# Other piece widths for the channel-major products, a norm split in two, and an output projection in three PSUM banks

## The chip, the cores and the metric

The kernel runs on one core of a Trainium2 chip. The metric is the device time of one execution in microseconds. TensorE is called PE here, VectorE DVE, ScalarE ACT, GpSimd POOL, and SyncE, whose queue issues nearly all DMA transfers, SP.

## The reference

One layer of a hybrid decoder for 1024 prompt tokens and 8 × 8 sample tokens (1088 in all), with model width 1024:

```python
h = rmsnorm(x, g_mix);  proj = h @ w_in            # 1024 -> 3328 columns
o_rw = rwkv7_mixer(...)       # 4 heads of 64: token shift, low-rank gates, matrix-state recurrence, bonus
o_cv = short_conv_mixer(...)  # pb * conv3(pc * px), 256 channels
o_sb = stick_breaking(...)    # 8 heads of 64; sample tokens attend to a paged cache of 512 as well
x = x + concat(o_rw, o_cv, o_sb) @ w_out
h2 = rmsnorm(x, g_mlp)
x = x + square(relu(h2 @ w_up)) @ w_down           # 1024 -> 4096 -> 1024
gate = sigmoid(rmsnorm(x, g_ple) @ w_ple_gate)
x = x + gate * (p @ w_ple_proj)                    # p: 256 wide, one row for each token
```

The new keys, values, recurrence states, shift rows and convolution rows are outputs too.

## The kernel before

All large products take fp32 operands split into a high part (fp32r) and the rest, and each k-step is three matmuls: high × high, high × low, low × high (L169 to L171 in `gemm_t`, L795 to L797 in `project`, L1094 to L1096 in `gemm_p`). ACT makes the high part with a cast, POOL or DVE the low part with a subtraction: for weights that is L158 and L159 in the first half, L1074 and L1075 in the second.

**First half, products by channel.** The loop at the start normalizes x tile by tile (128 tokens; h is L193), transposes it on PE (L198) and evicts the high part on ACT (L200) and the low part on DVE (L201). A channel-major product (`gemm_t`) makes 128 channels for all 1088 tokens, weights stationary. It goes in three pieces, given by `CH`, each with a PSUM bank of its own and 24 matmuls:

```python
CH = ((0, 384), (384, 384), (768, 320))
```

`rw_tile` does that for the eight 128-channel tiles of the recurrence and evicts each piece with L330 (copy) and L333 (scaled copy); the convolution does it for six. The low-rank gates, the squared norms of kk and the bonus of the recurrence use the same pieces. The bonus is L446 (a product with a block of ones) and L447 (the product times vx, in place in xs), three of each in a row. `wkv_base` solves the triangular systems of the recurrence on DVE: it loads base_Z from DRAM (L277) and goes through steps of L284 and L286. Its result is stored (L288), and each chunk of the recurrence loads its operands ar and bk (L487, L490) and then multiplies them (L512).

**First half, products by token.** `project` makes queries, keys and values: two token tiles with 256 columns each in one bank. ACT copies the bank (L802) and squares it into sq (L805, one buffer), and DVE makes the norms. L848 and L849 split and L852 stacks rows in DRAM; L828 stores keys.

**Second half.** Tokens 0 to 511 are group A, 512 to 1087 group B (two chunks of 288). A `Part` holds the residual x of a group. `out_proj` multiplies with w_out, 24 matmuls a piece, and DVE adds each piece to x (L1406). The order is: A's MLP blocks up to 13, `out_proj(B)`, A's last blocks, B's MLP with seven products of halves in place of eight (`seven`, L1446 to L1448), then A's gates in the loop over `gate(A, sl)`, between whose pieces B's operands are made, and last B's gates (`gate7`; L1596 to L1599 in `gated`).

`Part.rms` makes 1/rms of a group's tokens: ACT squares the eight slices of x, POOL and DVE add them up (L1329), DVE adds the last two (L1330, the tile `sums`); PE sums over the partitions with one-column matmuls (L1338), ACT and DVE take root and reciprocal, and PE (L1347) and ACT spread them over all partitions into `rb`. Each gate is multiplied with rb first (L1596). `ple_inputs` loads the rows of p (L1583), transposes them (L1586) and splits them. `gate7_weights` loads the weights of B's gates and makes their sums of blocks on DVE (L1430 to L1433).

**What sets the order.** A scheduler places the instructions when the program is built: each engine has one queue and goes through it in order, and the scheduler fills the queues by the order of the code and by times that it simulates for each instruction. A size that changes moves instructions far from its own line. PSUM has eight banks, and `banks(...)` hands out the named ones in turn; `acc` is banks 0, 1 and 2.

Of the kernel before, what the change touches and what calls it, by code (L numbers as in the profile page):

```python
# [33 lines left out]
NJ = 8  # L34
NS = NB * NJ
T = NP + NS
CH = ((0, 384), (384, 384), (768, 320))
C0 = math.exp(-0.5)
RMS_EPS = 1e-6
GN_EPS = 64e-5  # L40
# [8 lines left out]
def hybrid_step(ctx: ExitStack, tc: tile.TileContext, I, O):  # L49
# [6 lines left out]
    def f(t):  # L56
        return t.bitcast(F32)
# [9 lines left out]
    def banks(*ids):  # L67

        turn = itertools.cycle(ids)

        def take():
            i = next(turn)
            return psum.tile([128, 512], F32, name=f"b{i}", bufs=1)

        return take
# [67 lines left out]
    class Weights:  # L143
# [3 lines left out]
        def load(self, src, nk=8, ncol=256, tag="w", sub=None):  # L147
            wh = self.pool.tile([128, nk * ncol], F32R, name="wh", tag=tag + "h", bufs=2)
            wl = self.pool.tile([128, nk * ncol], F32R, name="wl", tag=tag + "l", bufs=2)
            wh3, wl3 = (w[:, :nk * ncol].rearrange("p (k c) -> p k c", k=nk) for w in (wh, wl))  # L150
            step = max(1, 1024 // ncol)
            for k0 in range(0, nk, step):
                n = min(step, nk - k0)
                raw = self.pool.tile([128, 1024], F32, name="wr", bufs=2)
                r3 = raw[:, :n * ncol].rearrange("p (k c) -> p k c", k=n)
                SP.dma_start(r3, src[k0 * 128:(k0 + n) * 128, :].rearrange("(k p) c -> p k c", p=128))
                flat = slice(k0 * ncol, (k0 + n) * ncol)
                S.copy(wh[:, flat], raw[:, :n * ncol])  # L158
                (sub or G).tensor_sub(wl[:, flat], raw[:, :n * ncol], f(wh[:, flat]))  # L159
            return wh3, wl3  # L160
# [67 lines left out]
    for s in range(2):  # L228
        hs = slice(64 * s, 64 * s + 64)
        for q in range(2):  # L230
            for kind in range(2):
                m = mfull[hs, q, kind, :]
# [86 lines left out]
    def rw_tile(w, m, ct):  # L319
# [5 lines left out]
        G.tensor_copy(rs3[:, :, 0], shT[:, ct, :])  # L325
        for t0, n in CH:
            ps = acc()
# [16 lines left out]
    def lora(dst, i, j, prods, func, bias):  # L344
        c = slice(j * 128, j * 128 + 128)
        for t0, n in CH:
            ps = tr()
# [29 lines left out]
    for j in range(2):  # L377
# [14 lines left out]
        for a in range(2):  # L392
            rb = pe_tile("rb", F32R)
            rbs.append((rb, rp.tile([128, 2, 64], F32R, name=f"rb8{a}")))
            for d, i0, i1 in ((rb[:, :1024], 0, 8), (rbs[a][1].rearrange("p s d -> p (s d)"), 8, 9)):
# [4 lines left out]
                else:  # L400
                    h = rbs[0][0][:, :1024] if i0 == 0 else rbs[0][1].rearrange("p s d -> p (s d)")
                    V.tensor_sub(d, src, f(h).rearrange("p (i s d) -> p i s d", i=i1 - i0, s=2))
        for t0, n in CH:
            ps = tr()
# [38 lines left out]
        SP.dma_start(ar_s[2, j], vx[:, t_])  # L443
        for t0, n in CH:
            ps = tr()
# [529 lines left out]
    def convolution():  # L975
# [5 lines left out]
        for j in range(2):  # L981
            t = cv.tile([128, LW], F32, name="cc", bufs=2)
            cc.append(t)
            for t0, n in CH:
                ps = gemm_cv()
# [4 lines left out]
        for j in range(2):  # L990
# [6 lines left out]
            S.copy(us3[:, :, 0:2], pt[:, :16].rearrange("p (b i) -> p b i", i=2))  # L997
            for t0, n in CH:
                ps = gemm_cv()
# [89 lines left out]
    def gemm_p(ps, w, m, x, t0, n, nk=8, ks=None):  # L1089

        xh, xl = x
        for k in ks or range(nk):
            a, b = xh[k // 4][:, k % 4, t0:t0 + n], xl[k // 4][:, k % 4, t0:t0 + n]
            PE.matmul(ps[:, :n], w(0, k, m), a, start=(k == 0), stop=False)  # L1094
            PE.matmul(ps[:, :n], w(0, k, m), b, start=False, stop=False)  # L1095
            PE.matmul(ps[:, :n], w(1, k, m), a, start=False, stop=(k == nk - 1))  # L1096
# [167 lines left out]
    class Part:  # L1264
# [56 lines left out]

        def rms(self, bank, wide=False):

            sums, sq = self.act("sums", F32), [self.act("sq", F32) for _ in range(2)]
            for m in range(8):
                t = sums[:, m] if m < 2 else sq[m // 2 % 2][:, m % 2]
                S.square(t, self.x[:, m])
                if m >= 2:
                    (G, V)[m % 2].tensor_add(sums[:, m % 2], sums[:, m % 2], t)  # L1329
            V.tensor_add(sums[:, 0], sums[:, 0], sums[:, 1])  # L1330
            self.rb = self.pool.tile([128, self.n], F32, name="rb", bufs=1)
            if not wide:

                n, ni = self.n, len(self.tiles)
                ps = bank()
                for i in range(ni):
                    e = min(n, 128 * i + 128)
                    PE.matmul(ps[:, i:i + 1], sums[:, 0, e - 128:e], onesq[:, 0:1], start=True, stop=True)  # L1338
                rs = self.pool.tile([128, ni], F32, name="rs", bufs=2)
                S.activation(rs, ps[:, :ni], AF.Sqrt, bias=eps_rms, scale=1.0 / D)  # L1340
                V.reciprocal(rs, rs)
                for t0 in range(0, n, 512):
                    r = min(512, n - t0)
                    ps = bank()
                    for i in range(t0 // 128, -(-(t0 + r) // 128)):
                        c = min(128, n - 128 * i)
                        PE.matmul(ps[:, 128 * i - t0:128 * i - t0 + c], rs[:, i:i + 1].to_broadcast([128, 128]),  # L1347
                                  ident[:, 128 - c:], start=True, stop=True)
                    S.copy(self.rb[:, t0:t0 + r], ps[:, :r])
            else:  # L1350
                for t0, n in self.chunks:
                    ps = bank()
                    PE.matmul(ps[:, :n], onesq, sums[:, 0, t0:t0 + n], start=True, stop=True)
                    S.activation(self.rb[:, t0:t0 + n], ps[:, :n], AF.Sqrt, bias=eps_rms, scale=1.0 / D)
                    V.reciprocal(self.rb[:, t0:t0 + n], self.rb[:, t0:t0 + n])
# [41 lines left out]
    def out_proj(p, k0=0, nk=8, bank=acc, order=None):  # L1397
        nm = 16 // nk
        x = [h[k0 // 4:] for h in p.h]
        for m0 in order or range(0, 8, nm):  # L1400
            w = load(w_out[k0 * 128:(k0 + nk) * 128, m0 * 128:(m0 + nm) * 128], nk, nm * 128)
            for m in range(m0, m0 + nm):
                for t0, n in p.chunks:
                    ps = bank()
                    gemm_p(ps, w, m - m0, x, t0, n, nk=nk)
                    V.tensor_add(p.x[:, m, t0:t0 + n], ps[:, :n], p.x[:, m, t0:t0 + n])  # L1406

    def up(p, fb, bank=acc):
        w = load(w_up[:, fb * 256:fb * 256 + 256], 8, 256)
        ah, al = p.act("ah", F32R), p.act("al", F32R)  # L1410
        for m in range(2):
            for t0, n in p.chunks:
                ps = bank()
                gemm_p(ps, w, m, p.h, t0, n)
                r = p.tmp("r")
                V.scalar_tensor_tensor(r[:, :n], ps[:, :n], 0.0, p.rb[:, t0:t0 + n], op0=ALU.max, op1=ALU.mult)
                S.square(r[:, :n], r[:, :n])
                S.copy(ah[:, m, t0:t0 + n], r[:, :n])
                V.tensor_sub(al[:, m, t0:t0 + n], r[:, :n], f(ah[:, m, t0:t0 + n]))  # L1419
        return p, fb, ah, al  # L1420
# [119 lines left out]
    B = Part(mpb, mpb, mpb, 512, 576, ((0, 288), (288, 288)))  # L1540
# [6 lines left out]
        u, before = up(A, fb), u  # L1547
        down(*before)
    late = banks(0, 1, 2, 3, 4, 5)
    out_proj(B, bank=late, order=(0, 4, 2, 6))  # L1550
    u, before = up(A, NA - 1, late), u
    down(*before, bank=late)
    B.rms(banks(6, 7))
# [74 lines left out]
    def gate(p, sl):  # L1628
        w = load(wg_[:, sl * 256:sl * 256 + 256], 8, 256)
        w2_ = load(wp_[:, sl * 256:sl * 256 + 256], 2, 256)  # L1630
        if sl == 3:

            ps_ = [acc() for _ in range(2)]
            for ks in (range(0, 4), range(4, 8)):
                for m2 in range(2):
                    gemm_p(ps_[m2], w, m2, p.h, 0, p.n, ks=ks)
        for m2 in range(2):
            for t0, n in p.chunks:
                if sl == 3:
                    ps = ps_[m2]  # L1640
                else:
                    ps = acc()
                    gemm_p(ps, w, m2, p.h, t0, n)
                end = gated(p, w2_, m2, 2 * sl + m2, t0, n, ps[:, :n], B.tmp("g")[:, :n])
            finish(p, 2 * sl + m2)
            yield end
# [46 lines left out]
    for m, end in enumerate(itertools.chain.from_iterable(gate(A, sl) for sl in range(4))):  # L1693
        with tc.issue_after(end.ins):
            if m < 3:
                B.operands("g_ple", (2, 3, 1, 4), mpb, 4, ks=((0, 1), (2,), (3,))[m], out=ops)
            if m == 2:
                B.rms(banks(3, 4))
            if m == 3:
                ple_inputs(B, banks(5, 7))  # L1700
        if m == 6:
            w = {}
            pieces = gate7_weights(0, w)
            for _ in range(5):
                next(pieces)
# [38 lines left out]
```

## Time and profile before

| | us |
|---|---|
| median of 3 runs (1706.22 to 1711.11) | 1706.24 |
| the profiled execution | 1715.32 |
| its span | 1713.5 |
| PE busy | 1641.7 |
| DVE, ACT, POOL busy | 1106.7, 821.3, 726.1 |

The span runs from the first instruction to the last; the rest of the profiled execution's time lies outside of it. Rows of a timeline give the start in us, the duration in us, the engine, the line, the operation, output and inputs with their shapes, and in brackets the idle time of the engine just before with what ended it. Matmuls overlap, so the pace of PE is read from start to start. A row "PE b L795 <- ACT sq L805: 5.4, 1, 5.4" says that PE waited for that ACT instruction 5.4 us in all, once, and 5.4 at the longest.

### The profile page before, as it was taken

Reading aid. Unit: us, or ns where it says so; the run is one execution under the profiler, and the core shown is the slowest. Engines: PE = TensorE matmul, PEld = TensorE weight load, DVE = VectorE, ACT = ScalarE, POOL = GpSimd, SP = SyncE. Lnnn points to the kernel's source line nnn. Section 1 sums busy time; section 2 is a strip of 40 time slices with the busy share of each in tenths; the row PEclk is TensorE's granted clock in tenths of the full one; section 3 lists DMA queues with packets and bytes.
Section 4 is the critical chain, followed back from the end, with each engine's and each line's share of the span. In section 5 each row is a group of like instructions: output and inputs, shape, how many; then the busy total and the mean of one; then the engine's idle time right before and its main releaser. Section 6 shows DMA issues by size and latency. Waiting matters only on the chain. (4 is left out here: it accounts for less than half of the span.)

```text
span 1713.5 us, 30844 instructions
## 1 busy us (share of the span) xinstructions
PE 1641.7 (96%) x11853; PEld 1479.4 (86%) x11853; DVE 1106.7 (65%) x1918; ACT 821.3 (48%) x1627; POOL 726.1 (42%) x778
## 2 busy tenths in 40 slices
PE   6999999999999898999999999999999999999998
PEld 5899988889888777888886777987999999999788
DVE  6266844555267759888854335277777777765896
ACT  6633433344344657666643344473443334437653
POOL 4123121123132565443334564366655455538631
PEclk9999999999999999999999999999999999999999
DMA  5134466335523764444235565322332322323332
GB/s 189 51 117 126 142 166 166 72 83 137 169 62 102 219 182 125 117 131 124 77 107 173 159 179 173 127 86 83 90 94 81 98 87 87 100 74 105 88 118 55
DMA packets 212373, 202.27 MB, mean 118 GB/s; under 512 B 58305, under 2 KB 177761, under 8 KB 212098
## 3 DMA queue, kind: packets, MB, share of 16 engines
q1 hardware_dynamic: 202498, 179.33, 35.4%
q0 software_dynamic: 5120, 16.78, 3.4%
q10 hardware_dynamic: 4608, 4.20, 1.0%
q8 instruction: 93, 1.52, 0.4%
q14 instruction: 54, 0.44, 0.1%
HBM read 163.27 MB, written 36.98 MB: 117 GB/s over the span
## 5 line engine op out<-in xcount | busy, mean ns | idle before, releaser
L1075 POOL TENSOR_TENSOR wl<-wr,wh 128x512 fp32r<-128x512 f32 x182 | 256.1, 1418 | 261.8 <-ACT wh L1074 208.5
L1074 ACT CAST wh<-wr 128x512 fp32r<-128x512 f32 x308 | 187.9, 621 | 310.9 <-PE b L1095 211.3
L1515 DVE TENSOR_TENSOR x<-b,x 128x288 f32<-128x288 f32 (+1 forms) x384 | 199.5, 529 | 96.4 <-PE b L1096 95.1
L1094 PE MATMUL b<-ah,wh 128*128 128x288 f32 (+1 forms) x768 | 253.8, 331 | 3.2 <-DVE x L1515 2.2
L1096 PE MATMUL b<-ah,wl 128*128 128x288 f32 (+1 forms) x768 | 252.6, 329 | 0.0
L1095 PE MATMUL b<-al,wh 128*128 128x288 f32 (+1 forms) x768 | 252.4, 329 | 0.0
L1094 PEld LDWEIGHTS b<-ah,wh 128*128 128x128 f32 x768 | 144.5, 188 | 15.4 <-DVE x L1515 4.6
L1096 PEld LDWEIGHTS b<-ah,wl 128*128 128x128 f32 x768 | 144.7, 188 | 10.2
L1095 PEld LDWEIGHTS b<-al,wh 128*128 128x128 f32 x768 | 144.8, 189 | 9.3 <-DVE al L1419 0.3
L795 PE MATMUL b<-wh,h_hi 128*128 128x256 f32 x432 | 128.2, 297 | 5.4 <-ACT sq L805 5.4
L1094 PE MATMUL b<-nh,wh 128*128 128x512 f32 x320 | 128.2, 401 | 2.8 <-DVE x L1406 1.6
L797 PE MATMUL b<-wh,h_lo 128*128 128x256 f32 x432 | 127.6, 295 | 0.0
L1095 PE MATMUL b<-nl,wh 128*128 128x512 f32 x320 | 127.4, 398 | 0.0
L1096 PE MATMUL b<-nh,wl 128*128 128x512 f32 x320 | 127.3, 398 | 0.0
L796 PE MATMUL b<-wl,h_hi 128*128 128x256 f32 x432 | 125.4, 290 | 0.0
L1075 DVE TENSOR_TENSOR wl<-wr,wh 128x512 fp32r<-128x512 f32 x126 | 105.2, 837 | 27.3 <-ACT wh L1074 24.4
L159 POOL TENSOR_TENSOR wl<-wr,wh 128x1024 fp32r<-128x1024 f32 x26 | 64.5, 2495 | 126.3 <-ACT wh L158 126.3
L169 PE MATMUL b<-h_hi,wh 128*128 128x384 f32 (+1 forms) x336 | 115.3, 343 | 1.9 <-ACT xs L333 1.3
L170 PE MATMUL b<-h_lo,wh 128*128 128x384 f32 (+1 forms) x336 | 114.2, 340 | 0.3 <-DVE h_lo L201 0.3
L171 PE MATMUL b<-h_hi,wl 128*128 128x384 f32 (+1 forms) x336 | 112.9, 336 | 0.0
L922 DVE TENSOR_TENSOR_SCAN keep<-keep,onesq 128x128 f32<-128x128 f32 (+3 forms) x64 | 95.6, 1494 | 21.4 <-POOL keep L920 20.7
L1446 PE MATMUL b<-op,wh 128*128 128x288 f32 x320 | 95.0, 297 | 3.1 <-DVE c L1596 1.8
(437 smaller groups left out, 4451.7 us busy)
## 6 DMA issues: line engine op xcount, KB each, us to landing
wr<-in_w_up SPq DMA_DIRECT2D x64, 512.0 KB
wr<-in_w_down SPq DMA_DIRECT2D x64, 512.0 KB
wr<-in_w_in SPq DMA_DIRECT2D x26, 512.0 KB
wr<-in_w_out SPq DMA_DIRECT2D x16, 512.0 KB
wr<-in_w_ple_gate SPq DMA_DIRECT2D x16, 512.0 KB
xt<-in_x_prompt SPq DMA_DIRECT2D x8, 512.0 KB
stk_s<-sth ACTq DMA_DIRECT2D x32, 128.0 KB
stk_s<-stl SPq DMA_DIRECT2D x32, 128.0 KB
```

The lines of the kernel that those rows point to most:

```text
L169: PE.matmul(ps[:, :n], wh[:, k, c], a, start=(k == 0), stop=False)
L170: PE.matmul(ps[:, :n], wh[:, k, c], b, start=False, stop=False)
L171: PE.matmul(ps[:, :n], wl[:, k, c], a, start=False, stop=(k == nk - 1))
L795: PE.matmul(o, a, w[0][:, k, :], start=(k == 0), stop=False)
L796: PE.matmul(o, a, w[1][:, k, :], start=False, stop=False)
L797: last = PE.matmul(o, b, w[0][:, k, :], start=False, stop=(k == 7))
L1074: S.copy(h3, src)
L1075: (sub or G).tensor_sub(l3, src, f(h3))
L1094: PE.matmul(ps[:, :n], w(0, k, m), a, start=(k == 0), stop=False)
L1095: PE.matmul(ps[:, :n], w(0, k, m), b, start=False, stop=False)
L1096: PE.matmul(ps[:, :n], w(1, k, m), a, start=False, stop=(k == nk - 1))
L1515: V.tensor_add(p.x[:, m, t0:t0 + n], ps[:, :n], p.x[:, m, t0:t0 + n])
```

## The change

Three edits. `CH` becomes pieces of 256, 384 and 448 tokens. `rms` is split into `squares()`, up to `sums`, and `spread()`, the rest; in the loop over A's gates, B's `squares()` stay at piece 2, and `spread()` and `ple_inputs(B)` come at piece 4 (`rms` stood at 2, `ple_inputs` at 3). `out_proj(B)` uses the three banks of `acc` and no longer the six of `late`, whose rotation then begins with `up` behind it. Lines from 1330 on move by 4 to 8.

```diff
-CH = ((0, 384), (384, 384), (768, 320))
+CH = ((0, 256), (256, 384), (640, 448))
...
         def rms(self, bank, wide=False):
 
+            self.spread(self.squares(), bank, wide)
+
+        def squares(self):
+
             sums, sq = self.act("sums", F32), [self.act("sq", F32) for _ in range(2)]
...
             V.tensor_add(sums[:, 0], sums[:, 0], sums[:, 1])
+            return sums
+
+        def spread(self, sums, bank, wide=False):
             self.rb = self.pool.tile([128, self.n], F32, name="rb", bufs=1)
...
-    out_proj(B, bank=late, order=(0, 4, 2, 6))
+    out_proj(B, order=(0, 4, 2, 6))
...
             if m == 2:
-                B.rms(banks(3, 4))
-            if m == 3:
+                sums = B.squares()
+            if m == 4:
+                B.spread(sums, banks(3, 4))
                 ple_inputs(B, banks(5, 7))
```

PE at the start: the end of the first product piece (bank b_416), the transposes of token tiles 3 to 5 (L198) and the head of the second piece (b_444). Before:

```order
L171 MATMUL b_416<-h_hi_81,wl 128x384
L198 MATMUL b_236<-ident,h 128x128 x4
L198 MATMUL b_243<-ident,h 128x128 x4
L198 MATMUL b_259<-ident,h 128x128 x4
L198 MATMUL b_266<-ident,h 128x128 x4
L198 MATMUL b_280<-ident,h 128x128 x4
L198 MATMUL b_287<-ident,h 128x128 x4
L169 MATMUL b_444<-h_hi_80,wh 128x384
```

And now:

```order
L171 MATMUL b_416<-h_hi_81,wl 128x256
L198 MATMUL b_236<-ident,h 128x128 x4
L198 MATMUL b_243<-ident,h 128x128 x4
L198 MATMUL b_259<-ident,h 128x128 x4
L198 MATMUL b_266<-ident,h 128x128 x4
L169 MATMUL b_444<-h_hi_80,wh 128x384
L198 MATMUL b_280<-ident,h 128x128 x4
L198 MATMUL b_287<-ident,h 128x128 x4
```

The first piece is narrower, and the second begins before the last pair of transposes.

DVE in the second head pair of the recurrence (near 170 us in the trace): L430 to L440 make operands, L284 and L286 are the first steps of `wkv_base`, L447 is the bonus, with vx in xs_1514. Before:

```order
L440 SCALAR_TENSOR_TENSOR xs_1412<-xs_1412,par_349,xs_1128 128x1088
L284 TENSOR_TENSOR base_Q_1329<-base_Z_1327,base_X_1328 128x31
L286 TENSOR_TENSOR base_X_1328<-base_X_1328,base_Q_1329 128x31
L284 TENSOR_TENSOR base_Q_1329<-base_Z_1327,base_X_1328 128x60
L286 TENSOR_TENSOR base_X_1328<-base_X_1328,base_Q_1329 128x30x2
L447 TENSOR_TENSOR xs_1412<-b6_1607,xs_1514 128x384
L284 TENSOR_TENSOR base_Q_1329<-base_Z_1327,base_X_1328 128x87
L447 TENSOR_TENSOR xs_1412<-b7_1610,xs_1514 128x384
L286 TENSOR_TENSOR base_X_1328<-base_X_1328,base_Q_1329 128x29x3
L447 TENSOR_TENSOR xs_1412<-b3_1613,xs_1514 128x320
```

And now:

```order
L440 SCALAR_TENSOR_TENSOR xs_1412<-xs_1412,par_349,xs_1128 128x1088
L447 TENSOR_TENSOR xs_1412<-b6_1607,xs_1514 128x256
L447 TENSOR_TENSOR xs_1412<-b7_1610,xs_1514 128x384
L447 TENSOR_TENSOR xs_1412<-b3_1613,xs_1514 128x448
L284 TENSOR_TENSOR base_Q_1329<-base_Z_1327,base_X_1328 128x31
L286 TENSOR_TENSOR base_X_1328<-base_X_1328,base_Q_1329 128x31
```

The three L447 stand ahead of the first L284. On PE their matmuls (L446) move up by 8 of the L795 to L797 matmuls around them, and the first L512 of the recurrence moves down by 46 of these.

SP some 40 us later, where the first chunk's operands are loaded (L487, L490). Before:

```order
L828 DMA out_2<-kg_3480 128x2x256
L288 DMA t_s_74<-base_X_1328 128x2048
L852 DMA stk_s_67<-stl_3551 64x2x256 x2
L487 DMA ar_1627<-ar_s_63 128x3x64 x2
L490 DMA ar_1627<-ar_s_63 128x2x64 x3
L487 DMA bk_1628<-bk_s_64 128x2x64 x2
```

And now:

```order
L852 DMA stk_s_67<-stl_3551 64x2x256 x2
L828 DMA out_2<-kg_3541 128x2x256
L288 DMA t_s_74<-base_X_1328 128x2048
L852 DMA stk_s_67<-stl_3626 64x2x256 x2
L487 DMA ar_1627<-ar_s_63 128x3x64 x2
L490 DMA ar_1627<-ar_s_63 128x2x64 x3
L487 DMA bk_1628<-bk_s_64 128x2x64 x2
```

A store of keys (kg_3541) and the next stacking (stl_3626) now stand ahead of the loads.

PE in A's gates (after 1600 us), around the one-column matmuls of B's norm (L1338, now L1345). Before:

```order
L1094 MATMUL b0_18524<-nh1_17989,wh_18469 128x512
L1095 MATMUL b0_18524<-nl1_17991,wh_18469 128x512
L1338 MATMUL b3_18353<-onesq_115,sums_18334 128x1 x5
L1096 MATMUL b0_18524<-nh1_17989,wl_18470 128x512
L1094 MATMUL b1_18595<-nh0_17988,wh_18571 128x512
```

And now, 36 rows further down:

```order
L1095 MATMUL b0_18596<-nl0_17990,wh_18575 128x512
L1345 MATMUL b3_18469<-onesq_115,sums_18334 128x1 x5
L1096 MATMUL b0_18596<-nh0_17988,wl_18576 128x512
L1615 MATMUL b6_18561<-ident_104,x_6827 128x128 x4
L1593 MATMUL b5_18491<-ident_104,pn_18489 128x128 x2
L1593 MATMUL b7_18498<-ident_104,pn_18496 128x128 x2
```

The norm's matmuls come a gate piece later, and the transposes of p (L1593) directly behind them.

## The prediction

> **What bounds the kernel now.** I read busy times first, then the clock, PE's waits, the windows around the longest of them, and last the timelines at three places.
>
> ```profile
> PE 1641.7 (96%) x11853; PEld 1479.4 (86%) x11853; DVE 1106.7 (65%) x1918; ACT 821.3 (48%) x1627; POOL 726.1 (42%) x778
> core 0: 1713.5 us, clock 0.985
> PE b L795 <- ACT sq L805: 5.4, 1, 5.4
> PE b L942 <- DVE beta L924: 3.5, 1, 3.5
> PE b L1338 <- DVE sums L1330: 3.4, 1, 3.4
> PE b L512 <- DMA bk<-bk_s: 2.2, 2, 2.0
> ```
>
> PE is busy 96%, no other engine above 65%. To be won are PE's idle time, 1713.5 − 1641.7 = 71.8 us in many small pieces (the waits: total, times, longest), and time at a low clock: (1 − 0.985) × 1713.5 = 25.7 us of its pace.
>
> ```profile
> 173.20:180.00 6.80, 5.30 (x25) 5.30 (x26) 6.42 (x23) 3.14 (x5) 0.00 (x0) 0.50 0.60 210
> 1613.60:1620.40 6.80, 5.93 (x19) 5.16 (x20) 3.50 (x6) 1.13 (x3) 0.37 (x2) 0.50 0.53 155
> 430.00:760.00 330.00, 308.26 (x1882) 262.96 (x1881) 232.03 (x385) 184.57 (x378) 141.09 (x219) 0.97 0.46 138
> 1080.00:1120.00 40.00, 40.00 (x305) 39.53 (x304) 11.80 (x24) 16.68 (x29) 15.24 (x12) 1.00 0.28 83
> 1640.00:1660.00 20.00, 16.87 (x123) 16.08 (x122) 20.00 (x34) 9.73 (x20) 7.42 (x5) 1.00 0.40 113
> ```
>
> After length come busy times of PE, PEld, DVE, ACT, POOL, then the clock. Around the 5.4 and the 3.4 us wait it is 0.50 for 6.8 us, so such a wait is paid twice.
>
> **The widths: 0 by themselves.**
>
> ```profile
> 168.91 0.28 PE L796 MATMUL b<-wl,h_hi 128*128 128x256 f32 x1
> 169.03 0.28 PE L797 MATMUL b<-wh,h_lo 128*128 128x256 f32 x1
> 24.85 0.33 PE L170 MATMUL b<-h_lo,wh 128*128 128x384 f32 x1
> 25.02 0.34 PE L171 MATMUL b<-h_hi,wl 128*128 128x384 f32 x1
> 1610.45 0.40 PE L1094 MATMUL b<-nh,wh 128*128 128x512 f32 x1
> 1610.69 0.40 PE L1095 MATMUL b<-nl,wh 128*128 128x512 f32 x1
> ```
>
> From start to start 0.12, 0.17 and 0.24 us for 256, 384 and 512 columns, nearly a line; by it 320 takes 0.147 and 448 0.20. Columns (1088) and number of matmuls stay, so the sum does. The change acts through the order.
>
> **The start: 1.5 us (0 to 5).**
>
> ```profile
> 17.61 1.94 PE L198 MATMUL b<-ident,h 128*128 128x128 f32 x8 [2.24 <-DVE h L193]
> 28.59 1.29 DVE L201 TENSOR_TENSOR h_lo<-b,h_hi 128x512 fp32r<-128x512 f32 x2 [2.05 <-ACT h_hi L200]
> 30.63 0.44 PE L169 MATMUL b<-h_hi,wh 128*128 128x384 f32 x1 [0.63 <-ACT h_hi L200]
> ```
>
> The first piece runs from those transposes to its last matmul at 25.02; 24 matmuls narrower by 128 columns save 24 × 0.05 = 1.2 us, more at half clock. But the second piece starts at 30.63, after ACT's and DVE's evictions, which piece widths don't hasten. So the first saving is covered; what stays is that later transposes come a little sooner. Ends: 0 (all covered), and 5: both waits shown (2.24 + 0.63) and twice the 1.2. I take 1.5, nearer the covered end.
>
> **The projection at 170 us: 7.5 us (3 to 9).**
>
> ```profile
> 163.32 1.35 DVE L440 SCALAR_TENSOR_TENSOR xs<-xs,par 128x1088 f32<-128x1088 f32 x1
> 171.37 0.19 DVE L284 TENSOR_TENSOR base_Q<-base_Z,base_X 128x31 f32<-128x31 f32 x1 [6.70 <-DMA base_Z<-l_s]
> 173.48 0.48 DVE L447 TENSOR_TENSOR xs<-b,xs 128x320 f32<-128x320 f32 x1
> 174.05 0.60 ACT L805 ACTIVATE sq<-b 128x512 f32<-128x512 f32 x1 [11.69 <-DMA wr<-in_w_in]
> 166.25 1.99 PE L446 MATMUL b<-xs,bones 128*128 128x384 f32 x6
> 174.70 0.58 PE L795 MATMUL b<-wh,h_hi 128*128 128x256 f32 x1 [5.38 <-ACT sq L805]
> ```
>
> ACT's release is named as a DMA, but sq starts right behind the last L447 (173.96), whose source vx lies where sq is put. The L447s, their matmuls done at 168.24, stood on DVE's in-order queue behind L284, which waited until 171.37 for base_Z. In the new order all three stand ahead of it. L446 moves 8 matmuls up PE (8 × 0.12 = 1.0 us), so ends at 167.3; the last L447 ends some 0.7 later, sq at 168.6. PE has 17 matmuls (2.0 us) until it needs the bank, 169.3: slack 0.7. So the wait of 5.38 goes, and with it the half-clock window: 5.30 busy at 0.50 lose 2.65. Together 8.0.
>
> What is late next: the base_Z load now stands behind a 512 KB weight load on SP, but only L284 waits for it. The chunk loads that the recurrence's L512 needs are the next wait:
>
> ```profile
> 207.21 0.19 DVE L286 TENSOR_TENSOR base_X<-base_X,base_Q 128x31 f32<-128x31 f32 x1
> 212.53 1.24 SPq L852 DMA_DIRECT2D stk_s<-stl  x2
> 215.70 0.69 DVE L849 TENSOR_TENSOR stl<-nat,sth 128x512 fp32r<-128x512 f32 x1 [0.54 <-ACT sth L848]
> 217.69 1.15 SPq L490 DMA_DIRECT2D bk<-bk_s  x2
> ```
>
> On SP two more DMAs stand ahead of them, a store of keys and the stacking of stl, whose L849 ended at 216.4. It follows PE, 8 us earlier, so 208.4, or the end of DVE's chain (207.2) and what is queued behind: about 210. Loads follow 6 us after L852, so bk lands about 2.5 us sooner. PE puts L512 behind 46 more matmuls (5.5 us), so it arrives 8 − 5.5 = 2.5 us sooner: the 2.0 us wait stays. I take off 0.5. The low end, 3: chunk loads no earlier, wait 5 us longer. The high one, 9: the wait at L512 goes as well.
>
> **Attention and convolution, 430 to 760: 0 (−5 to +5).** Pieces and chunks are reordered throughout. PE idles 330 − 308.3 = 21.7 us there and loses 0.03 × 330 = 9.9 to the clock. In the order I find moves of both signs; a sixth of this either way is my bound.
>
> **Output projection in three banks: 0 (−1 to +1).**
>
> ```profile
> L1406 DVE TENSOR_TENSOR x<-b,x x16: 443/458/458, 1079.6 to 1124.4; 128x288 f32<-128x288 f32 x16
> 1703.28 0.29 PE L1094 MATMUL b<-ph,wh 128*128 128x288 f32 x1
> 1703.41 0.29 PE L1095 MATMUL b<-pl,wh 128*128 128x288 f32 x1
> ```
>
> A piece is 24 × 0.13 = 3.1 us; its bank is freed by one L1406 of 0.46 and is needed again two pieces, 6.2 us, later. The margin is 5.8 us, DVE is busy 11.80 of 40, and PE has no gap to lose. If the cover went (DVE held up over 5.8 us), PE would wait the rest.
>
> [...] The window at 1080 shows clock 1.00 while cycling six banks; three are not shown.
>
> **The gates: 5 us (2 to 9).**
>
> ```profile
> 1612.03 1.77 POOL L1075 TENSOR_TENSOR wl<-wr,wh 128x512 fp32r<-128x512 f32 x1
> 1612.78 1.63 DVE L1330 TENSOR_TENSOR sums<-sums 128x576 f32<-128x576 f32 x1
> 1617.61 0.69 DVE L1430 TENSOR_TENSOR s<-wr 128x512 f32<-128x512 f32 x1 [3.19 <-DMA wr<-in_w_ple_gate]
> 1614.47 2.29 PE L1338 MATMUL b<-onesq,sums 128*128 128x1 f32 x10 [3.38 <-DVE sums L1330]
> ```
>
> The column sums move 36 rows down PE's order, 36 × 0.23 = 8.3 us. DVE's adds move back too, and two block sums (L1430, L1432) now stand ahead of the last ones. They wait for weights, whose loads come ahead of the p rows on SP and whose POOL splits now precede the adds. POOL has the same work before its last add as before, so ends it by 1613.8, and L1330's end falls at 1615 to 1617, before PE at 1618.9. The 3.38 us go, and half of 5.93, 3.0, of low clock: 6.4. Behind, DVE is full (20.00 of 20 at 1640): its 3.19 us of idle now take work from there, but ple_inputs come later. I take off 1.4. Low end 2: the wait moves to 1640; high end 9: the 3.1 us that PE idles at 1640 shrink too.
>
> **Sum:** 1.5 + 7.5 + 0 + 0 + 5 = 14.0 against the profiled 1715.3 (span 1713.5), which is 9.1 above the median 1706.24. Of its 25.7 us of low clock the median run may lack those 9.1, a third; of my sum 5.6 are low clock, so 2 come off: 12 us, **1694**.
>
> **Rivals.**
> - The recurrence takes back the gain at 170 us. Its chain, not PE, sets the pace from 200 to 280: for it the two DMAs put ahead on SP; against it, PE's own wait there is only 2.2 us. Gain 5: 1701. Chance 0.13.
> - The gates give all back, as DVE has no idle to lend at 1640 (for: 20.00 of 20; against: 3.19 idle at 1617): gain 7 or 8, 1698. Chance 0.12. [...]
> - The middle falls well too: 7 us more, 1687. Chance 0.10.
> - Slower: the third piece. It is now the widest and ends 24 × (0.20 − 0.147) = 1.3 us later against its tile's start; where what follows waits for the tile's end, each of 14 tiles (8 recurrence, 6 convolution) pays it: 18 us, so 1706 − 12 + 18 = 1712. It decides once over 9 of 14 tiles pay. Against: PE's groups run from tile to tile, and waits ahead of L169 don't rank among its long ones. Chance 0.07.
> - Three banks hold PE up: half of each L1406 seen, 16 × 0.23 = 4 us: 1698; or worse. Chance 0.04.
> - Nothing stays: moves cancel, 1706. Chance 0.09.
>
> The forecast has 0.45, its own range 1689 to 1699. Change under 0.3% (5.1 us) can't be told from none: faster is 0.45 + 0.12 + 0.10 + 0.03 + half of the first rival = 0.76; slower 0.07; the same 0.17. Ends of the terms reach 28 us up (1678) and 1 down; leaving out the last 2 in 10, range 1682 to 1706.
>
> **What would show it.** Right: no wait of L795 for sq near 170 and clock 1.00 there; L512 waits about 2 us; no wait for sums near 1610; 1080 to 1120 still full at clock 1.00; PE's idle near 62 us. Wrong: a wait over 5 us before L512, DVE idle less but PE's waits at 1640 to 1700 longer, or idle in 430 to 760 above 27 us.

## The result: slower, and the profile after

The changed kernel takes 1723.87 us (median of 4 runs, 1720.48 to 1727.78) against 1706.23 for the kernel before on the same chip: a ratio of 1.0098, 95% interval 1.0079 to 1.0117. I had forecast 1694 and held slower for 7 in 100. The main term, the wait near 170 us, and the bound on the middle, from 430 to 760 us, were both wrong.

The page of the changed kernel, first its cores, then the busy times, then PE's waits (in total, times, longest), and last its window from 430 to 760 us (PE's busy time after the length, the clock third from the end):

```profile
core 0: 1725.0 us, clock 0.982
PE 1650.8 (96%) x11853; PEld 1479.5 (86%) x11853; DVE 1111.0 (64%) x1918; ACT 820.7 (48%) x1627; POOL 728.5 (42%) x778
PE b L844 <- DVE nat L810: 4.3, 1, 4.3
PE b L942 <- DVE wtl L61: 3.6, 1, 3.6
PE b L577 <- DVE Wm L570: 3.1, 1, 3.1
PE b L512 <- DMA bk<-bk_s: 2.7, 2, 1.7
PE b L1615 <- ACT yt L1616: 2.7, 1, 2.7
PE b L169 <- ACT cc L987: 2.3, 1, 2.3
430.00:760.00 330.00, 302.72 (x1837) 256.27 (x1836) 221.24 (x374) 175.08 (x359) 135.81 (x212) 0.95 0.45 135
```

Both waits that I had set out to see gone are gone: L795 for sq (5.4) and the squares' L1338 for sums (3.4; now L1345 waits 1.0, for g). In their place stand three that were short before: L844 (the transposes of nat, the normalized queries and keys) waited 0.5 us, L942 (the attention's transposes of beta) waited for wtl 1.7 us in three waits, and L577 (the recurrence's product with Wm) 0.4 us. PE idles 1725.0 − 1650.8 = 74.2 us, not 62, and from 430 to 760 us it idles 27.3 us, just over the 27 that I had named as a sign of being wrong, at clock 0.95, not 0.97.

To see where the time went, the executions are cut at equal amounts of PE's work (each matmul counted by its spacing, 0.12, 0.17 and 0.23 us for 256, 384 and 512 columns). The measure of "before" is the kernel with three banks alone (e3). The first 7,500 rows of its PE order, up to 1074 us, are those of before, and its profiled execution lies at its median (1711.17 against 1711.13), where that of before lies 9 us above its own. In the recurrence the execution of before has 6.8 us of half clock (279.0 to 285.8 us, clock 0.50) and a wait of 1.3 us that e3 lacks. The names of the experiments are explained below; the times of the stretches on the clock are e3's.

| stretch (us in e3) | before | e3 | after | e1 widths | e2 spread | e4 recurrence | e5 tiles | e6 sums | e7 convolution | e8 sequence |
|---|---|---|---|---|---|---|---|---|---|---|
| 8–260 | 252.5 | 251.9 | 251.0 | 247.0 | 255.0 | 251.6 | 250.9 | 253.9 | 253.6 | 250.3 |
| 260–423, recurrence | 167.2 | 162.7 | 173.2 | 174.7 | 163.1 | 173.5 | 166.4 | 166.8 | 163.1 | 166.5 |
| 423–547 | 125.1 | 124.1 | 125.7 | 126.7 | 124.1 | 124.0 | 122.7 | 122.5 | 125.0 | 121.5 |
| 547–601, attention | 53.7 | 53.8 | 62.8 | 59.5 | 53.8 | 59.6 | 59.7 | 58.1 | 54.8 | 58.9 |
| 601–721 | 118.6 | 119.8 | 120.6 | 120.9 | 121.2 | 123.1 | 122.9 | 119.6 | 125.8 | 119.3 |
| 721–1116 | 396.7 | 395.6 | 393.6 | 393.5 | 393.4 | 393.2 | 392.9 | 394.1 | 393.1 | 393.8 |
| 1116–1565 | 449.2 | 448.5 | 448.5 | 449.3 | 448.3 | 448.3 | 448.4 | 449.0 | 448.4 | 448.4 |
| 1565–1704, gates | 137.4 | 139.4 | 136.9 | 137.4 | 131.9 | 136.7 | 137.3 | 136.1 | 136.5 | 136.7 |

After against e3: −0.9, **+10.5**, +1.6, **+9.0**, +0.8, −2.0, 0, −2.5, in all 16.5 us. A stretch whose order is the same repeats within 4.5 us from one execution to the next (before, e2 and e3 up to 721 us), so the two in bold are the loss. In the recurrence, 2.9 us of it are longer waits, 1.7 us a low clock, and 6 us PE's own pace, with neither. In the attention, some 5 us are waits and 3.4 us low clock, and the pace is that of e3.

The recurrence was dearest in the three kernels with the new widths in all of its products (after, e1, e4); e5, e6 and e8 lose some 4 us there. The attention was dear in every kernel with another order in the recurrence, by 4 to 9 us, also in e6, whose tiles have the old widths, and in e8, which has no new width at all. The convolution's stretch (601–721) was dearest in e7; after and e1 have its widths too and lose 1 us there.

This division has a flaw: it counts a small matmul too low, one of 128 columns with some 0.07 us, where the transposes of this size are spaced 0.11 (16 of L198 in 1.91 us from 23.50 on in after, 20 in 2.34 from 25.20 on in before). Divided by the spacing that each form of small matmul has in the kernels of the old order, the recurrence of after takes 171.6 us and the stretch ahead of it 253.7, so that some 2 of the 10.5 us belong ahead of the recurrence; the attention's loss becomes 8.4.

### The profile page after: what moved, and what is told of

It reads as the page before. It is cut to its first block, busy times and chain, and to the rows that moved or that the text cites. A ratio compares the mean times of both kernels' runs of the same rounds, so it can differ in the third digit from the quotient of the medians.

```text
span 1725.0 us, 30839 instructions
## 1 busy us (share of the span) xinstructions
PE 1650.8 (96%) x11853; PEld 1479.5 (86%) x11853; DVE 1111.0 (64%) x1918; ACT 820.7 (48%) x1627; POOL 728.5 (42%) x778
## 5 line engine op out<-in xcount | busy, mean ns | idle before, releaser
L1095 PE MATMUL b<-al,wh 128*128 128x288 f32 (+1 forms) x768 | 251.6, 328 | 0.5 <-DVE al L1426 0.5
L1096 PE MATMUL b<-ah,wl 128*128 128x288 f32 (+1 forms) x768 | 251.9, 328 | 0.0
L795 PE MATMUL b<-wh,h_hi 128*128 128x256 f32 x432 | 127.6, 295 | 0.0
L797 PE MATMUL b<-wh,h_lo 128*128 128x256 f32 x432 | 126.9, 294 | 0.0
L169 PE MATMUL b<-h_hi,wh 128*128 128x256 f32 (+2 forms) x336 | 116.4, 347 | 5.5 <-ACT h_hi L200 2.4
L1075 DVE TENSOR_TENSOR wl<-wr,wh 128x512 fp32r<-128x512 f32 x126 | 100.4, 798 | 26.2 <-ACT wh L1074 25.3
L159 POOL TENSOR_TENSOR wl<-wr,wh 128x1024 fp32r<-128x1024 f32 x26 | 65.5, 2534 | 120.2 <-ACT wh L158 120.2
L171 PE MATMUL b<-h_hi,wl 128*128 128x256 f32 (+2 forms) x336 | 115.5, 344 | 0.0
L170 PE MATMUL b<-h_lo,wh 128*128 128x256 f32 (+2 forms) x336 | 115.0, 342 | 0.0
```

The costliest lines, as they stand in the source:

```text
L169: PE.matmul(ps[:, :n], wh[:, k, c], a, start=(k == 0), stop=False)
L170: PE.matmul(ps[:, :n], wh[:, k, c], b, start=False, stop=False)
L171: PE.matmul(ps[:, :n], wl[:, k, c], a, start=False, stop=(k == nk - 1))
L795: PE.matmul(o, a, w[0][:, k, :], start=(k == 0), stop=False)
L797: last = PE.matmul(o, b, w[0][:, k, :], start=False, stop=(k == 7))
L1075: (sub or G).tensor_sub(l3, src, f(h3))
```

## The experiments

Two theories stood at the start. S: a few waits that the trace names carry the loss, and each has its own cause. R: the order of the first half is fragile, and any new order costs some us, wherever it comes from. Each part of the change was run alone first.

**e1, the widths alone** (old gates, six banks):

```
-CH = ((0, 384), (384, 384), (768, 320))
+CH = ((0, 256), (256, 384), (640, 448))
```

> Only the widths 256, 384, 448; norm and output projection as before. Theory A (the widths reorder the first half, and the loss arises before 1068 us; in the trace of the changed kernel PE's lag behind the kernel before is 16 us at 760 and 12 us from 800 on, and hardly moves behind that): 1718 to 1724, slower by 12 to 17 us. Rival B (the gates: the new waits of L1615 for L1606 and its neighbours, 2.7 and 2.5 us with half-clock windows, are the loss): 1706 to 1711. Rival C (three banks): 1706 to 1711.

1721.07, ratio 1.0083 (1.0062 to 1.0104), as theory A had it. The widths carry most of the loss.

**e2, the squares spread later, alone:**

```
             if m == 2:
-                B.rms(banks(3, 4))
-            if m == 3:
+                sums = B.squares()
+            if m == 4:
+                B.spread(sums, banks(3, 4))
```

> Only the split norm and the later p inputs; widths and banks as before. Theory A: 1703 to 1709, since the lag gains 4 us at the sums, loses 7 behind them and gets 3 back. Rival B: 1713 or more. My prediction's own term: 1701 (5 us faster).

1699.80, ratio 0.9960 (0.9943 to 0.9976): faster by some 6.8 us, 5.5 of them in the gates' stretch (137.4 to 131.9). That is my own term and not theory A. It is the best version of this case, faster than both kernels.

**e3, three banks alone:**

```
-    out_proj(B, bank=late, order=(0, 4, 2, 6))
+    out_proj(B, order=(0, 4, 2, 6))
```

> Only the output projection in three banks. Theory A and my prediction's term: 1706, within 1 us. Rival C (banks cycled too fast, PE idles between pieces or its clock falls): over 1710.

1711.13, ratio 1.0021 (1.0007 to 1.0035). The projection itself, from its first eviction to its last, took 46.7 us rather than 44.8 (1.3 of it one wait for xr that now falls into it), and the gates, 400 us behind it, 139.4 rather than 137.4. That is more than the 1 us expected, but not by the mechanism of rival C: PE idles 1.3 us at that one wait, and the clock from 1080 to 1130 us is 1.00.

**e4, the new widths in everything but the convolution, e7 in the convolution alone** (its three loops read a second table):

```
+CHC = ((0, 384), (384, 384), (768, 320))     # e4, with the new widths in CH; in e7 the other way round
-            for t0, n in CH:
+            for t0, n in CHC:
```

> New widths in the recurrence's tiles, low-rank gates, kk and bonus only; convolution at 384, 384, 320; norm and banks as before. Theory A1 (the waits of the first 430 us and of the convolution each carry about half: L577 waits 3.1 us at 357 with a half-clock window, base_Z comes 4.8 us later): 1711 to 1715. Rival A2 (the convolution alone carries the loss, its 256 piece leaving PE without a bank at 446): 1704 to 1708. Rival A3 (any new order of the first half costs the attention's part its fit): 1715 to 1722.

> New widths in the convolution alone, which cycles two banks. Theory S: the piece of 256 leaves PE without a bank near 445 for 2 us (L169 waits for ACT's L987), with a half-clock window 4 us in all: 1706 to 1711. Rival A2 (the convolution carries most of the loss): 1714 or more. Rival A4 (its widths cost nothing of their own): 1704 to 1707, no wait of L169 for L987.

e4 1721.94, ratio 1.0073 (1.0045 to 1.0102); e7 1714.55, 1.0038 (1.0024 to 1.0052). Either alone costs. Their sum, 1.0111, lies above e1, which has both (1.0083), but within the noise of e4 it can't be told whether they add. e4 is in the range of rival A3 and e7 in that of A2, so the convolution costs something too, but less than the rest. In e7 the wait for sq near 170 us is still there (5.3).

**e5, the new widths in the eight projections of rw_tile alone; e6, in the bonus sums L446 and L447 alone:**

```
+CHN = ((0, 256), (256, 384), (640, 448))
-        for t0, n in CH:      # e5: in rw_tile;  e6: the loop around L446
+        for t0, n in CHN:
```

> New widths in the eight recurrence tiles alone (gates, kk, bonus, convolution, norm and banks as before). Here too the three L447 stand ahead of L284, but base_Z is loaded behind one weight load, not two, and L512 stands where it stood. Theory S (named waits carry the loss: base_Z late, L512 and the chunk's loads late, the DVE stall at 357): the wait near 170 goes or is under 2 us, and the time is 1698 to 1706. Rival R (any new order of the first half costs some 10 us, whichever): 1712 to 1722.

> New widths in the bonus alone: L446 and L447, 2 x 3 instructions. The L447s stay among the L284s, while some 3000 rows of PE's order differ from 500 on. Theory S: 1703 to 1709. Rival R: 1712 to 1722.

e5 1716.44, 1.0060 (1.0040 to 1.0081), with the wait for sq gone and a wait of L844 for nat of 4.5 us in its place. e6 1713.56, 1.0036 (1.0020 to 1.0053), with the wait for sq still there. Three small multiplications of other widths in each of two head pairs, with no change of the work, cost 6 us. Theory S missed in e5, in e6 and, above, in e7, each of which took longer than its range; R's 1712 to 1722 holds e5 and e6.

**e8, the old widths in another order**, 384, 320, 384 in all loops but one:

```
+CHN = ((0, 384), (384, 320), (704, 384))
```

> The widths of before, 384, 384, 320, in another sequence (384, 320, 384) everywhere but in kk: the same instructions but for the place of the 320, and another order. Theory S: what the order happens to do, 1702 to 1712. Rival R: 1712 to 1722. Rival W (the width of 448 or 256 is what costs): 1706, within 3.

1710.13, 1.0010 (1.0000 to 1.0019). So R in its strong form (every new order costs 10 us) fell: reorderings of the first half cost from 2 to 14 us. Its weak form stands, as each of them costs something.

**e9, the wait for sq taken away with the order held.** My main term was a claim on one wait, so it was tried by itself. In the kernel of e2 the second tile's vx is touched first, by which it takes another buffer, and the sq of the projection no longer lies on it:

```
         xs = pe_tile("xs")
+        if xs_first:
+            G.memset(xs[:, T:T + 1], 0.0)
```

> The kernel of the spread alone (old widths, six banks), with vx of the second tile written first (one added memset of 128x1 on POOL), so that it takes another buffer and the squares sq of the projection no longer lie on it. The order of every instruction on PE, ACT, DVE and SP is the same as in the spread alone; only the wait of L795 for sq near 170 us is taken away, without any width. My prediction's step (P): the 5.4 us and half of its half-clock window go, 7.5 us, so 1692 against 1699.8 for the spread alone, ratio 0.9915. Theory M, the wait only moves: the landing of base_Z holds L284 until about 172 as before, behind it on DVE stand L807 and L810, L810 starts at about 182, and L844 on PE, which now arrives some 8 us early, waits for it; L844 starts at 182.5 to 183 against 183.3. Then the gain is 0 to 1.5 us: 1698 to 1700, ratio 0.995 to 0.996, and a wait of L844 for nat of 4 to 7 us stands in the place of the one for sq.

1703.46 against 1708.56 for before on that chip, ratio 0.9963 (0.9947 to 0.9979), where e2 had 0.9960 (0.9943 to 0.9976): nothing was won that can be measured. Timelines of e2 (first row) and of e9 near 170 to 190 us, start and duration, in brackets the idle time and its releaser (e9's lines count two more), and e9's window with PE's busy time first and the clock as the third number from the end:

```profile
175.78 0.58 PE L795 MATMUL b<-wh,h_hi 128*128 128x256 f32 x1 [5.70 <-ACT sq L805]
173.91 0.19 DVE L284 TENSOR_TENSOR base_Q<-base_Z,base_X 128x31 f32<-128x31 f32 x1 [6.49 <-DMA base_Z<-l_s]
183.00 0.68 DVE L812 TENSOR_TENSOR nat<-nat,ss 128x512 f32<-128x512 f32 x1
183.74 1.12 PE L846 MATMUL b<-ident,nat 128*128 128x128 f32 x4 [6.02 <-DVE nat L812]
182.60:189.40 6.80, 5.66 (x27) 5.66 (x28) 6.53 (x16) 2.58 (x5) 0.00 (x0) 0.53 0.02 4
```

In e2 PE stands 5.70 us at L795; in e9 it passes there and stands 6.02 us at L846 (L844 in the other kernels), with low clock behind in both (0.61 from 174.3 to 181.1 us in e2, 0.53 from 182.6 to 189.4 in e9). In e2 L844 waits another 1.5 us, so the two kernels wait 7.2 and 6.0 us in all. DVE comes to the norm of nat when base_Z has landed and the chain from L284 has run: its product starts 9.4 us behind L284 in e2 (172.45 to 181.88) and 9.1 in e9. Theory M is shown; my step (P) is refuted.

**e10, POOL's splits near 590 us given to DVE** in the changed kernel. The edit takes eight, the four meant (588.0 to 594.5 us) and the next four, up to 608 us; POOL has 244 of these splits left out of 252:

```
-            w = load(w_out[...], nk, nm * 128)
+            w = load(w_out[...], nk, nm * 128, sub=V if p is A and k0 == 0 else None)
```

> The changed kernel, with four of POOL's weight splits (L1075, those that ran from 588.0 to 594.5 us) done by DVE instead. PE's order is the same as in the changed kernel up to about 575 us, and differs behind. Theory N (named waits): POOL holds DVE's operations there, o comes late, and through SP's queue the weight loads and L942; without POOL's instructions the 3.6 us wait of L942 and its half clock go: the stretch that took 62.8 us (553 to 616) comes to 55 to 58, and the total to 1717 to 1719, ratio 1.006. Theory R (any new order costs its own amount): the stretch may shrink, but other waits come in behind, and the total stays at 1722 to 1727, ratio 1.010 to 1.012.

1719.02, ratio 1.0057 (1.0040 to 1.0073), against 1.0098 of the changed kernel. The stretch came from 62.8 to 54.9 us, the 53.8 of before within its scatter, and the wait of L942 for wtl left it. N is borne out, though the run doesn't separate the first four splits from the next; of the 7.9 us that the stretch gained, some 5 to 7 reached the total.

**e11, the changed kernel without its widths** (spread and three banks):

> Old widths, the squares spread later, and the output projection in three banks: the changed kernel without its widths. If the parts add (spread 0.9960, three banks 1.0021): 0.998, 1703. If the three banks undo the spread, as the gates of the changed kernel against the widths alone suggest (its stretch 136.9 against 137.4 us, where the spread alone had 131.8 against 137.4): 1707 to 1710, ratio 1.001 to 1.002.

1708.09, ratio 0.9996 (0.9976 to 1.0015), between the two expectations. The gates took 136.1 us, against 131.9 with six banks: the three banks take back 4.2 of the 5.5 us that the spread wins.

**e12, POOL beside DVE by themselves:**

> A small program by itself that computes nothing of the reference: five phases of 40 DVE instructions in a row on one 128x256 tile (product of two SBUF tiles, TENSOR_SCALAR of 128 columns, copy SBUF to SBUF, product of PSUM and SBUF, copy from PSUM), alone; beside 16 subtractions of 128x1024 on POOL; beside 16 copies on POOL; beside 16 memsets on POOL; beside 16 copies on ACT. Theory H (POOL's instruction holds DVE's SBUF instructions until it ends): beside the subtractions the SBUF instructions take up to 2.4 us, on average over 1 us, rather than 0.2 to 0.5, and those that read PSUM alone stay as they are; beside ACT nothing changes. [...]

Its timeline, POOL's 16 subtractions as one row (2.43 us each), one round of DVE beside them, and one after POOL's end:

```profile
21.08 38.93 POOL L83 TENSOR_TENSOR wl<-wr,wl 128x1024 f32<-128x1024 f32 x16
29.42 1.60 DVE L64 TENSOR_TENSOR x<-x,one 128x256 f32<-128x256 f32 x1
31.05 2.25 DVE L65 TENSOR_SCALAR x<-x,col 128x128 f32<-128x128 f32 x1
33.33 2.45 DVE L66 COPY x<-x 128x256 f32<-128x256 f32 x1
35.82 0.42 DVE L67 TENSOR_TENSOR x<-b,x 128x256 f32<-128x256 f32 x1
36.28 0.42 DVE L68 COPY x<-b 128x256 f32<-128x256 f32 x1
61.95 0.42 DVE L64 TENSOR_TENSOR x<-x,one 128x256 f32<-128x256 f32 x1
62.41 0.34 DVE L65 TENSOR_SCALAR x<-x,col 128x128 f32<-128x128 f32 x1
62.79 0.29 DVE L66 COPY x<-x 128x256 f32<-128x256 f32 x1
```

H is right: beside the subtractions a DVE instruction from SBUF to SBUF lasts until POOL's instruction that was running ends, to 0.3 us (POOL's ends taken at its pace of 2.43), whatever it costs alone. There is no common factor: 0.42 becomes 1.60 (2.60 in the first round), 0.34 becomes 2.25 and 0.29 becomes 2.45, and the two that read PSUM take 0.42 in both. Beside POOL's copies (1.16 us each) the same three take 0.60, 0.94 and 1.13 in the mean (the product was held once in five times); beside its memsets the product stays at 0.42 and the other two take 0.56 and 1.04; beside ACT's copies nothing changes (0.42, 0.34 and 0.29).

## Why the prediction was wrong, step by step

**The widths by themselves: 0. Right for the wide matmuls.** 448 columns are spaced 0.20 us as forecast. The small matmuls of the recurrence did not keep their pace, though: with waits over 0.15 us and the loss to low clock taken off, the recurrence's stretch has some 6 us more in after than in e3 (4 by the second division above). This pace belongs to the order: it is 162.1 to 162.7 us in the six kernels with the old order there (before, e2, e3, e7, e9, e11), 165.9 in e5, e6 and e8, and 168.3 to 168.5 in after, e1 and e4. One group of it, the 128 L512 (busy, mean ns of one, idle before), in e3 and then in after:

```profile
L512 PE MATMUL b<-ar,bk 64*128 64x128 f32 x128 | 17.4, 294 | 2.3 <-DMA bk<-bk_s 2.3
L512 PE MATMUL b<-ar,bk 64*128 64x128 f32 x128 | 18.3, 290 | 2.7 <-DMA bk<-bk_s 2.7
```

The same number, the same form, 0.9 us more time on PE: what stands between them differs. That their neighbours set this pace is an inference; no run took apart which of them do.

**The start: 1.5 us. Not seen.** PE's wait for h_hi ahead of the second piece is 2.4 us now, where it was 0.6: that piece waits for the evictions, as said, and the saving is covered entirely.

**The projection at 170 us: 7.5 us. The step that failed is "but only L284 waits for it".** Everything ahead of that sentence came as written, within 1 us: the last L447 and sq moved up, and L795 no longer waits. The base_Z load did fall behind a weight load on SP. Timelines of the changed kernel, SP's queue, DVE, ACT and PE (start, duration), and the window of the low clock:

```profile
168.20 0.41 SPq L156 DMA_DIRECT2D wr<-in_w_in  x1
168.98 3.08 SPq L277 DMA_DIRECT2D base_Z<-l_s  x2
176.16 0.19 DVE L284 TENSOR_TENSOR base_Q<-base_Z,base_X 128x31 f32<-128x31 f32 x1 [6.83 <-DMA base_Z<-l_s]
180.07 0.68 DVE L810 TENSOR_TENSOR nat<-nat,ss 128x512 f32<-128x512 f32 x1
169.42 0.60 ACT L805 ACTIVATE sq<-b 128x512 f32<-128x512 f32 x1 [5.67 <-DVE xs L447]
180.81 1.11 PE L844 MATMUL b<-ident,nat 128*128 128x128 f32 x4 [4.35 <-DVE nat L810]
179.80:186.60 6.80, 5.79 (x27) 5.79 (x28) 6.49 (x20) 2.72 (x6) 0.00 (x0) 0.50 0.02 4
```

sq is written at 169.4, 4.6 us earlier than before. But its reduction L807 and the product L810 stand behind L284 on DVE's in-order queue, and L284 starts at 176.16, when base_Z has landed, 4.8 us later than before. In before, L810 stood here:

```profile
180.48 0.68 DVE L810 TENSOR_TENSOR nat<-nat,ss 128x512 f32<-128x512 f32 x1
```

It comes at 180.07 now, 0.4 us earlier. PE is ready for the transposes L844 at 176.46 (180.81 − 4.35) and waits for it. My working asked who waits for the load, and not what is queued behind the instruction that waits. e5 shows the same wait, and e9 shows that even with base_Z no later the 5.7 us only move from L795 to the next consumer. Nothing was to be won at this place by freeing the bank.

**Attention and convolution: 0 (−5 to +5). The term that was mis-sized, by more than double:** +11.4 from 423 to 721 us, +9.0 of it at 547–601. The recurrence ahead of it lost 10.5, for which I had provided 0.5 and a rival. Two waits there have a cause that the trace shows whole. At 357 us, in the changed kernel (L608 and L610 normalize the recurrence's output yc):

```profile
353.38 4.88 POOL L159 TENSOR_TENSOR wl<-wr,wh 128x1024 fp32r<-128x1024 f32 x2 [9.21 <-ACT wh L158]
353.91 2.14 DVE L608 TENSOR_TENSOR yc<-yc,sqy 128x256 f32<-128x256 f32 x1
356.09 2.51 DVE L610 TENSOR_SCALAR yc<-yc,par 128x128 f32<-128x128 f32 x2
359.61 0.41 DVE L570 COPY Wm<-b 128x256 f32<-128x256 f32 x1
360.07 0.65 PE L577 MATMUL b<-AB,Wm 64*64 64x128 f32 x8 [3.11 <-DVE Wm L570]
```

In the new order the weight split L159 falls beside L608 and L610, and L608 and the first of the two L610 end with one of its halves, as in e12; Wm's copy and PE stand behind. In the order of before L159 came later, and the two took 0.42 and 0.59:

```profile
352.31 0.42 DVE L608 TENSOR_TENSOR yc<-yc,sqy 128x256 f32<-128x256 f32 x1
353.24 0.59 DVE L610 TENSOR_SCALAR yc<-yc,par 128x128 f32<-128x128 f32 x2
359.23 4.70 POOL L159 TENSOR_TENSOR wl<-wr,wh 128x1024 fp32r<-128x1024 f32 x2 [3.77 <-ACT wh L158]
```

There the split fell beside evictions that read PSUM and a product, L849, that took 2.43 us without making PE wait. No run moved this split alone, but the kernels sort by it: in after, e1 and e4 it falls beside L608 and L577 waits 3.1 us; in e5, e6 and e8 it comes behind, L608 takes 0.41 and L577 waits 0.4. What this place costs is the wait and 3.4 us of half clock, so some 5 us. e12 shows the same by itself: a product of L608's size took 1.60 to 2.60 us beside POOL's subtractions and 0.42 alone. Not every POOL instruction did this: beside the memsets the product stayed at 0.42, and beside the copies at 0.42 to 0.43 in four of five (1.27 in the other). What decides it was not shown. I had counted busy shares of DVE and POOL and never asked what ran beside what.

At 588 to 606 us the same thing sets off a chain:

```profile
588.02 6.51 POOL L1075 TENSOR_TENSOR wl<-wr,wh 128x512 fp32r<-128x512 f32 x4 [1.75 <-ACT wh L1074]
589.94 1.78 DVE L924 TENSOR_TENSOR beta<-beta,keep 128x512 f32<-128x512 f32 x1
594.49 0.41 DVE L956 TENSOR_TENSOR o<-b,o 64x256 f32<-64x256 f32 x1
586.22 9.15 SPq L957 DMA_DIRECT2D mix_s<-o  x2
596.10 0.95 SPq L1068 DMA_DIRECT2D wr<-in_w_out  x2
604.54 1.14 ACT L1074 CAST wh<-wr 128x512 fp32r<-128x512 f32 x2 [3.23 <-DMA wr<-in_w_out]
606.32 0.58 PE L942 MATMUL b<-ident,beta 128*128 128x128 f32 x2 [3.56 <-DVE wtl L61]
```

POOL holds DVE's products (L924, 0.68 us at this size elsewhere, takes 1.78); the output o (L956) comes late; SP, in order, stands 9 us at its store L957; the weight load behind it is issued at 596.1; ACT waits for the weights, and behind that on ACT's queue stands the split of wth for which PE's next group waits. e10 took away the head of this chain and won back the stretch. A third wait, L169 for cc, 2.3 us, comes straight from the widths: the convolution's first piece is shorter, so PE comes to the third 7.1 rather than 8.3 us after its start, while ACT's eviction L987 is held until 448.2 by a store. e1 and e7, with the same piece, wait 1.4 and 1.5 us there, and e4 and e5, with the old one, not at all. What e7 loses at 601–721 (6 us: 2.4 of waits, 3.4 of low clock) was not traced to one cause.

**The output projection in three banks: 0 (±1). Right in its place, wrong in its reach.** The evictions of after, to be laid beside those of before in the prediction, and a window in their midst:

```profile
L1413 DVE TENSOR_TENSOR x<-b,x x16: 443/458/458, 1092.8 to 1137.6; 128x288 f32<-128x288 f32 x16
1090.00:1130.00 40.00, 40.00 (x306) 39.53 (x306) 11.17 (x23) 15.36 (x27) 14.46 (x11) 1.00 0.32 102
```

From the first to the last they take 44.8 us, as before, with PE full and the clock at 1.00.

What I left out is that other banks change the order of what follows: the gates (e3 against before, e11 against e2) pay 2 to 4 us. That is no more than one execution differs from the next, but the medians of e3 and of e11 against e2 show a cost too.

**The gates: 5 us (2 to 9). Right alone, by 6.8 us in e2,** and gone beside the three banks. PE's waits from 1590 us on, in e2 and then in after:

```profile
PE b L1615 <- DVE x L1606: 3.8, 2, 2.7
PE b L1615 <- DVE x L1606: 2.7, 2, 2.5
PE b L1615 <- ACT yt L1616: 2.7, 1, 2.7
```

The wait for sums went in both; with three banks a new one for yt comes (also in e3, 1.8, and in e11, 2.6, but not in before or e2).

**The sign.** The rival that ended slower, the wide third piece that delays 14 tiles, was not what happened: no wait ahead of L169 but that for cc grew in the middle. The nearest rival was the one in which the recurrence takes back the gain, at 13 in 100, and it took more than the gain. Every term of my sum was time that the diff removes; for what a new order creates I had only a symmetric bound. (The upper ends of my terms add up to 29 us, not 28; nothing hangs on it.) The runs show no symmetry: all eight kernels that reorder the first half (after, e1, e4 to e8, e10) came out slower, by 1.0010, whose interval touches 1, to 1.0098.

What stays open: what in the new order slows PE's own pace in the recurrence (4 to 6 us), why every new order there makes the attention wait, through other waits in e4, e5, e6 and e8 than in after, and e7's 6 us.

## What to carry to other kernels

When a wait is removed, list what stands behind the late instruction on its in-order queue, not only who reads its result: the next consumer may be held by the same late load, and then the wait moves and nothing is won (5.70 us at L795 in e2, 6.02 at L846 in e9). Where a scheduler rebuilds the order from sizes, try each part of a change alone, since here one part was worth 0.4% and another cost 0.8%. And look up, for each long POOL instruction, which DVE instructions from SBUF to SBUF run beside it (a product of 0.42 us took 1.60 in e12).

## What the runs showed of the hardware

Beside POOL's subtractions DVE was not slowed but held: a copy of 0.29 us took 2.45 (e12), so a small instruction cost what remained of POOL's 2.43.

What a wait costs in clock is not fixed. Behind the same wait at the same instruction, the low clock lasted 3.4 us in the changed kernel (0.50 from 360.7 to 364.1) and some 24 us in e10, whose windows are here (0.90 and 0.91 in the ten us ahead and behind):

```profile
357.91 1.11 PE L577 MATMUL b<-AB,Wm 64*64 64x128 f32 x8 [3.12 <-DVE Wm L570]
360.00:370.00 10.00, 10.00 (x65) 8.41 (x62) 2.08 (x6) 0.00 (x0) 0.00 (x0) 0.50 0.45 125
370.00:380.00 10.00, 10.00 (x62) 8.42 (x62) 2.98 (x9) 0.98 (x3) 0.00 (x0) 0.50 0.01 2
```

PE was busy all that time, at clock 0.50, and the stretch took 182.2 us against 173.2. e10's other runs, 1717 to 1722 us but for this one's 1726.65, suggest that this length is rare.
